# The lower part of split weights: from a subtraction on the vector engine to an accumulating DMA

## The chip, the cores and the metric

The kernel runs on one core of one Trainium2 chip. The metric is the time of an execution on the device, in microseconds (us); several executions are timed and the median stands for them.

## What is computed

Two transformer blocks follow each other over 512 tokens of 1024 features, all in float32:

```python
def reference(x, mem, ...):
    y = first_block(x, mem, ...)     # mixer, attention to 256 memory rows, gated FFN, norm
    return second_block(y, ...)      # stick-breaking attention + 31-tap conv, gated FFN

# first block
xn = rmsnorm(h, norm_mix_g);  proj = xn @ w_in
h = h + concat([pool_mixer(p), sgu_mixer(u, v)]) @ w_out
h = h + mem_cross_attention(rmsnorm(h, norm_xattn_g), mem, wq, wk, wv, wo)
h = h + (silu(gate) * val) @ w_down       # gate, val: a 3-tap convolution of xn @ w_up
# second block
proj = rms_norm(x) @ w_in_2               # q, k, v and the two halves of a gated unit
x = x + concat([attention(q, k, v), conv_branch]) @ w_out_2
x = x + (silu(conv(gate)) * val) @ w_down_2
```

What matters here is the products with weights: w_in, w_out, wq, wk, wv, wo, w_up, w_down and those of the second block, some 112 MB read once.

## The kernel before

**Products in three parts.** The matmuls take their operands in a rounded 32-bit type (`F32R`). To keep float32 accuracy, each operand is split in two, a rounded upper part `hi` and what the rounding left, `lo = raw - hi`. A product is then three matmuls into one PSUM tile, in `mm3` (L123 to L125): `wh*xh`, `wh*xl`, `wl*xh`.

**Weight units.** The weights are cut into units of 128 partitions x 2048 columns (8 KB to a partition, 1 MB in all), listed in `PLAN` in the order of use: 111 units, 8 of them with only 1536 columns (the last six of the 22 feature chunks of each down projection, `PARTS`), and three `EARLY` units that are split ahead into slots that lie free. A unit with 512 tokens takes 16 steps of `mm3`, 48 matmuls; one with 1536 columns takes 36.

**prep** (from L174) loads the next unit and splits it. Per unit:

```python
raw = wp.tile([P, UNIT], F32, tag="raw")      # pool wp: two buffers for each tag
hi = slot(..) if slots else wp.tile(.., tag="whi")
lo = slot(..) if slots else wp.tile(.., tag="wlo")
sp.dma_start(out=raw[:, cs], in_=wts[i][:, cs])                              # L190
act.copy(hi[:, cs], raw[:, cs])                                              # L197
dve.tensor_tensor(lo[:, cs], raw[:, cs], hi[:, cs].bitcast(F32), subtract)   # L198
```

Unit 0 is loaded in five pieces and its upper part is cast on VectorE (DVE, L195), with the parts of the first activations between the pieces. For all others ScalarE (ACT) casts, then DVE subtracts.

**weights** calls `prep` until two units are ready and gives out the first. So the split of unit n+1 stands in the program just ahead of the matmuls of unit n, and it writes into the whi and wlo buffers that unit n-1 used. Its raw buffer is loaded as soon as the split of unit n-1 has read it.

**Order of work.** The program is written stage by stage; each engine's order is set by a scheduler that runs a timeline of its own when the program is built (`schedule_with_timeline_sim`). An engine takes its instructions strictly in that order; each waits for its semaphores. SyncE's queue (SP) holds nearly only the weight loads. GpSimd (POOL) holds sums of squares for the norms (L301 to L305), small powers (L326, L739) and memsets in the feed-forward evacuation (L650, L992).

**Stages**, in order of time: pool and gating mixer; keys of the memory (wk); w_out; queries (wq); scores, values (wv), output (wo); feed-forward of block 1 (`ffn`: eight up units, eight up, four down, six up, four down, four down of 1536 columns, during which early units are split); gated unit, heads and convolution of block 2; attention; w_out_2; feed-forward of block 2. In an up stage the evacuation of a unit is one product on DVE (L651), taps on ACT and DVE (L128, L646), Silu (L656), a product (L657) and a split of the result (L131, L132).

Of the kernel before, what the change touches and what calls it, by code (L numbers as in the profile page):

```python
# [10 lines left out]
F32 = mybir.dt.float32  # L11
F32R = mybir.dt.float32r
AF = mybir.ActivationFunctionType
# [15 lines left out]
NWARM = 14  # L29
NFIRST = 56  # the columns of the small arrays that are needed first  # L30
PIECES = ((0, 1), (1, 2), (2, 4), (4, 6), (6, 8))


def _plan():
    """The weight units in the order in which they are used: (array, kind, place)."""
    plan = []
    plan += [("w_in", "sta", (2 * u, 2 * u + 1)) for u in range(2)]
    plan += [("w_in", "mov", (1024, 4 * h)) for h in range(2)]
    plan += [("w_in", "sta", (4 + 2 * u, 5 + 2 * u)) for u in range(2)]
    plan += [("wk", "sta", (2 * u, 2 * u + 1)) for u in range(4)]  # L40
    plan += [("w_out", "sta", (2 * u, 2 * u + 1)) for u in range(4)]
    plan += [("wq", "sta", (2 * u, 2 * u + 1)) for u in range(4)]
    plan += [("wv", "mov", (512 * c, 4 * h)) for c in range(2) for h in range(2)]
    plan += [("wo", "sta", (2 * u, 2 * u + 1)) for u in range(4)]

    def ffn(up, down):
        ups = [[(up, "sta", (i, NF + i)) for i in range(f0, f0 + n)] for f0, n in PARTS]
        dns = [[(down, "dwn", (2 * u, f0, n)) for u in range(4)] for f0, n in PARTS]
        return ups[0] + ups[1] + dns[0] + ups[2] + dns[1] + dns[2]

    plan += ffn("w_up", "w_down")
    glu = [[("w_in_2", "sta", (12 + i, 16 + i))] for i in range(4)]
    qkv = [[("w_in_2", "mov", (512 * c, 4 * h)) for h in range(2)] for c in range(3)]
    plan += glu[0] + glu[1] + glu[2] + qkv[1][1:] + glu[3] + qkv[2]
    plan += [("w_out_2", "hlf", (n0, k0)) for k0 in (0, 4) for n0 in (0, 4)]
    plan += ffn("w_up_2", "w_down_2")
    return plan, qkv[0] + qkv[1][:1]
# [18 lines left out]
def block_kernel(  # L76
# [20 lines left out]

# [1 line left out]
    def pair():  # L99
# [51 lines left out]
    class Chunks:  # L151
        """Chunks of w columns in 8 KB slots; a slice of chunks lies in one of them."""

# [16 lines left out]

# [1 line left out]
    state = {"next": 0, "ready": [], "bank": 0}  # L172

    def prep(pieces=((0, 8),), before=None, between=None, early=None, slots=None):  # L174
        """Loads and splits the next unit, or one of those that are split early into slots."""
        i = state["next"] if early is None else len(PLAN) + early
# [14 lines left out]
        for a, b in pieces:  # L191
            cs = slice(a * n // 8, b * n // 8)
            if between:
                between(a, b)
                dve.tensor_copy(hi[:, cs], raw[:, cs])  # L195
            else:
                act.copy(hi[:, cs], raw[:, cs])  # L197
            dve.tensor_tensor(lo[:, cs], raw[:, cs], hi[:, cs].bitcast(F32), ALU.subtract)  # L198
        if kind == "hlf":
# [14 lines left out]
    def sta_unit(xh, xl, nk=KC, apart=False):  # L214
        """Two 128-column tiles of a weight against the activations: out^T in a pair of banks."""
        wh, wl = weights()
        pt = [single() for _ in range(2)] if apart else pair()
        order = [(k, j) for j in range(2) for k in range(nk)]
        for k, j in order if apart else sorted(order):
            mm3(pt[j] if apart else pt[:, j, :], wh[:, k, j, :], wl[:, k, j, :], xh[:, k, :],  # L220
                xl[:, k, :], k == 0, k == nk - 1)
        return pt

    def mov_stage(xh, xl, nt, early=()):
        """512 columns of a weight against the activations: tokens on the partitions."""
        pts = [pair() for _ in range((nt + 1) // 2)]
# [11 lines left out]

# [1 line left out]
    sm = const.tile([P, NSMALL], F32, tag="sm", name="sm")  # L240
# [27 lines left out]
    dve.tensor_copy(identr, ident)  # L268
    # the tensor engine's clock rises with its use: keep it at work until the data comes
    warm = single()  # L270
    for _ in range(NWARM):
        pe.matmul(warm.rearrange("p (a b) -> p a b", a=4), negone, over2(negone, 4),
                  start=True, stop=True)
    # where a key is not before its query
    never = const.tile([P, P], F32R, tag="never", name="never")
# [5 lines left out]

# [1 line left out]
    class Stats:  # L283
        """Sums of squares over the features; parts of 1024 columns: n chunks of w tokens."""

# [43 lines left out]
    def spread(c, w=T):  # L329
        """Per-token numbers, a token to a partition, onto all partitions along the free axis."""  # L330
        nt = w // P
# [9 lines left out]

# [1 line left out]
    xh, xl = whole("B"), whole("C")  # L343
# [140 lines left out]
    def residual(xh, xl, nxt_h, nxt_l, g, nk=KC):  # L484
        """h += W^T x; the next stage's input and the sums of squares as the chunks come."""
        st = Stats()
# [11 lines left out]

# [1 line left out]
    qh, ql = whole("B"), whole("C")  # L500
# [94 lines left out]

# [1 line left out]
    def ffn(xh, xl, st, places, evacuate, finish, meanwhile=(), last=None):  # L597
# [83 lines left out]

# [1 line left out]
    cc = part(ht[0], 4, 544)  # L683
# [65 lines left out]

# [1 line left out]
    # one head pair: the logits lie transposed, keys on the partitions  # L751
    # a step takes one or two tiles of 128 keys; the columns of a tile are the queries from its
    # first key on
    STEPS = ((2, 3), (1,), (0,))
    WIDE = (384, 384, 512)

    def cols_of(a):
        """Where a tile's columns lie in its step."""
        at = 256 if a == 3 else 0
        return slice(at, at + T - a * P)  # L760
# [3 lines left out]
    def sticks(hp, n):  # L764
        """Logits of a step's keys and log(1 + e^z) of them, in two parts."""
        w = WIDE[n]
# [18 lines left out]
    def breaks(hp, n):  # L785
        """What is left of the stick at each key, and the values taken by it."""
        w = WIDE[n]
# [13 lines left out]
    def gather(hp):  # L801
        """The values of a head pair, weighted."""
        o = single(0)
# [8 lines left out]

# [1 line left out]
    done = [0] * 4  # L814
    tap = None

    def conv(n, *chunks):
        """The next n taps of some chunks, in turns: a sum's next term waits for the one before."""
        nonlocal tap
# [35 lines left out]
    def blk(hp, n):  # L855
        """Where the two parts of a step's log(1 + e^z) lie."""
        tl = place((hp % 2, 2, 3)[n])
        return tuple(part(tl, 2, WIDE[n], 2 * WIDE[n] * i) for i in range(2))

    def taken(hp, n):  # L860
        """Where a step's weights lie."""
        at = (0, 1024 * (hp % 2), 768)[n]
# [10 lines left out]
    def conv_norm():  # L873
        """The layer norm over the channels, and its output's two parts."""
        nonlocal cl
# [41 lines left out]
    def half_out(u, xh, xl, out, after=None):  # L917
        """Two column tiles of the output projection over four chunks of its input."""
        if u % 2 == 0:
# [25 lines left out]
    def project():  # L945
        """The values of all heads, a tile of tokens at a time."""
        ws = [weights() for _ in range(2)]
# [13 lines left out]
    for i, x in enumerate(seq):  # L961
        # a step's parts may be overwritten once the last step of the pair before has read them
        while todo < len(seq) and todo <= i + 2 and not (x[1] == 2 and seq[todo][1] == 1):
# [7 lines left out]
    conv_norm()  # L971
    # the tensor engine takes the norm's sums between these products
    after = (None, None, (marks[0], marks[1]), (marks[1], marks[2]))
# [45 lines left out]
def _pack(a):  # L1019
    """Inputs laid out for the kernel: transposed activations, weights in the order of use."""  # L1020
    a = {k: np.asarray(v) for k, v in a.items()}
# [77 lines left out]
```

## Time and profile before

| | |
|---|---|
| three runs | 1300.12, 1303.54, 1305.39 us; median 1303.54 |
| profiled execution: span from first to last instruction | 1301.2 us |
| TensorE matmul (PE), busy | 1282.9 us, 99% |
| VectorE (DVE) | 777.4 us, 60% |
| ScalarE (ACT) | 483.6 us, 37% |
| GpSimd (POOL) | 119.6 us, 9% |
| moved by DMA | 118.33 MB, mean 91 GB/s |
| mean granted TensorE clock | 0.990 |

The profiled execution is one more run of the same program; the page gives its span, which lies between the lowest and the median run. "PEld" in the profile is the load of the stationary operand, which overlaps PE. A busy share says how long an engine had an instruction in hand, not that it set the end; the chain of waits is there for that. Lines (L198) are those of the listing above.

### The profile page before, as it was taken

The page shows a single profiled execution, that of the slowest core. Times are in us where ns is not written, and L with a number is a line of the kernel's source. Part 1 is how long each engine was busy: PE and PEld are TensorE (multiplying, and loading weights), DVE is VectorE, ACT ScalarE, POOL GpSimd, SP SyncE. Part 2 cuts the span into 40 slices and gives each one's busy share as a digit, 9 for nine tenths or more (in the row PEclk, how much of TensorE's full clock was granted, in tenths as well). Part 3 has the DMA queues.
Part 4 walks back from the last instruction along what each step waited for, and adds up shares of the span by engine and source line. Part 5 has one row for each costly group of instructions (what it writes and reads, how often), then busy time and mean ns, then how long its engine had stood idle before and what let it go on. Part 6 is the DMA issues. An engine that isn't in the chain of part 4 may idle for free.

```text
span 1301.2 us, 13631 instructions
## 1 busy us (share of the span) xinstructions
PE 1282.9 (99%) x5712; PEld 1027.5 (79%) x5712; DVE 777.4 (60%) x811; ACT 483.6 (37%) x523; POOL 119.6 (9%) x132
## 2 busy tenths in 40 slices
PE   8999999999999999999999899999999999999998
PEld 5789888788888888888888687667878888888887
DVE  8755534744866664465476998766665555445522
ACT  5332424632544442333352225654433333223310
POOL 4100210012000000000064230000400000000000
PEclk9999999999999999999999899989999999999999
DMA  7223222312222222222442002001222222222222
GB/s 259 97 97 130 97 97 68 127 65 97 98 97 90 84 88 95 97 97 89 138 156 71 33 33 70 28 1 37 93 97 97 97 97 97 98 96 83 87 72 85
DMA packets 20446, 118.33 MB, mean 91 GB/s; under 512 B 2208, under 2 KB 4128, under 8 KB 7712
## 3 DMA queue, kind: packets, MB, share of 16 engines
q1 hardware_dynamic: 20096, 117.20, 25.9%
q8 instruction: 45, 0.74, 0.2%
q10 hardware_dynamic: 288, 0.26, 0.1%
q14 instruction: 17, 0.14, 0.0%
HBM read 115.35 MB, written 2.10 MB: 90 GB/s over the span
## 4 chain that ended last, share of the span: by engine, by line
PE 94%; DVE 3%; ACT 1%; POOL 1%; DMA 0%; issue 0%; SPq 0%; DVEq 0%; ACTq 0%
PE pp L123 29%; PE pp L124 28%; PE pp L125 28%; DVE H L828 1%; PE ps L124 1%; PE ps L123 1%; PE ps L125 1%; PE ps L809 1%; PE pp L794 1%; PE pp L797 1%; PE pp L776 1%; DMA raw<-in_wts 0%; POOL col L739 0%; PE ps L318 0%; DVE wlo L198 0%
## 5 line engine op out<-in xcount | busy, mean ns | idle before, releaser
L197 ACT CAST whi<-raw 128x2048 fp32r<-128x2048 f32 (+1 forms) x104 | 195.1, 1877 | 458.7 <-PE pp L124 376.3
L198 DVE TENSOR_TENSOR wlo<-raw,whi 128x2048 fp32r<-128x2048 f32 (+3 forms) x109 | 237.9, 2183 | 73.3 <-ACT whi L197 72.8
L124 PE MATMUL pp<-C,whi 128*128 128x512 f32 x672 | 266.2, 396 | 2.2 <-DVE C L140 2.1
L125 PE MATMUL pp<-B,wlo 128*128 128x512 f32 x672 | 266.3, 396 | 1.4 <-DVE wlo L198 1.2
L123 PE MATMUL pp<-B,whi 128*128 128x512 f32 x672 | 266.4, 397 | 0.6 <-DVE whi L195 0.4
L124 PE MATMUL pp<-G,whi 128*128 128x512 f32 x448 | 177.9, 397 | 0.0
L125 PE MATMUL pp<-F,wlo 128*128 128x512 f32 x416 | 165.0, 397 | 0.0
L123 PE MATMUL pp<-F,whi 128*128 128x512 f32 x416 | 164.2, 396 | 0.0
L124 PEld LDWEIGHTS pp<-C,whi 128*128 128x128 f32 x672 | 126.3, 188 | 34.8 <-DVE C L140 4.4
L125 PEld LDWEIGHTS pp<-B,wlo 128*128 128x128 f32 x672 | 126.2, 188 | 32.7 <-DVE wlo L198 2.3
L123 PEld LDWEIGHTS pp<-B,whi 128*128 128x128 f32 x672 | 126.3, 188 | 32.3 <-ACT B L139 1.3
L124 PEld LDWEIGHTS pp<-G,whi 128*128 128x128 f32 x448 | 84.2, 188 | 20.4 <-issue 0.5
L625 DVE TENSOR_TENSOR A<-pp,A 128x1024 f32<-128x1024 f32 x23 | 28.2, 1225 | 112.2 <-PE pp L125 112.2
L123 PEld LDWEIGHTS pp<-F,whi 128*128 128x128 f32 x416 | 78.2, 188 | 19.3 <-issue 0.2
L646 DVE SCALAR_TENSOR_TENSOR H<-H,sm,H 128x512 f32<-128x512 f32 x132 | 92.8, 747 | 0.7
L125 PEld LDWEIGHTS pp<-F,wlo 128*128 128x128 f32 x416 | 78.2, 188 | 18.9 <-issue 0.2
L828 DVE SCALAR_TENSOR_TENSOR H<-H,sm,H 128x512 f32<-128x512 f32 x120 | 90.3, 784 | 1.2
L651 DVE TENSOR_TENSOR H<-pp,rb 128x1024 f32<-128x1024 f32 x22 | 26.9, 1224 | 56.2 <-PE pp L125 49.9
L128 ACT ACTIVATE H<-H,sm 128x512 f32<-128x512 f32 x70 | 54.2, 807 | 7.5 <-DVE H L698 7.5
L993 DVE TENSOR_TENSOR H<-pp,rb 128x512 f32<-128x512 f32 x22 | 15.2, 692 | 67.6 <-PE pp L125 61.2
L124 PE MATMUL pp<-E,whi 128*128 128x512 f32 x112 | 44.4, 396 | 0.0
L123 PE MATMUL pp<-D,whi 128*128 128x512 f32 x112 | 44.2, 395 | 0.0
(295 smaller groups left out, 1881.1 us busy)
## 6 DMA issues: line engine op xcount, KB each, us to landing
raw<-in_wts SPq DMA_DIRECT2D x99, 1024.0 KB, 4.7
raw<-in_wts SPq DMA_DIRECT2D x8, 768.0 KB, 3.9
A<-in_xT SPq DMA_DIRECT2D x3, 512.0 KB, 6.8
out<-A SPq DMA_DIRECT2D x3, 512.0 KB, 2.8
D<-in_memT SPq DMA_DIRECT2D x1, 1024.0 KB, 10.8
raw<-in_wts SPq DMA_DIRECT2D x3, 256.0 KB, 7.0
A<-in_xT SPq DMA_DIRECT2D x2, 256.0 KB, 3.9
raw<-in_wts SPq DMA_DIRECT2D x2, 128.0 KB, 4.0
```

Of the source, the lines that this page charges most:

```text
L123: pe.matmul(out, wh, xh, start=start, stop=False, **kw)
L124: pe.matmul(out, wh, xl, start=False, stop=False, **kw)
L125: pe.matmul(out, wl, xh, start=False, stop=stop, **kw)
L128: act.activation(out, in_, AF.Identity, scale=scale, bias=bias)
L197: act.copy(hi[:, cs], raw[:, cs])
L198: dve.tensor_tensor(lo[:, cs], raw[:, cs], hi[:, cs].bitcast(F32), ALU.subtract)
L625: dve.tensor_tensor(hu, pt, hu, ALU.add)
L646: dve.scalar_tensor_tensor(dst, hs[:, k : k + 512], w(k), dst, ALU.mult, ALU.add)
L651: dve.tensor_tensor(hs[:, :, 2:], pt, over2(rb), ALU.mult)
L776: pe.matmul(out[:, :P], identr, never, start=False, stop=False, skip_group_check=True)
L828: tap = dve.scalar_tensor_tensor(cv[:, i, :], cc[:, i, k : k + 512], par("dw_w", 4 * k + i), cv[:, i, :], ALU.mult, ALU.add)
L993: dve.tensor_tensor(hs[:, 2:514], pt[:, 0, :], rb, ALU.mult)
```

## The change

In `prep`, on the branch that all units but unit 0 take, the subtraction on DVE goes. ACT writes the negated copy of the raw weights into lo, in the rounded type, so that lo holds -hi. ACT casts hi as before. Then POOL issues a DMA from raw to lo, both in SBUF, that adds what it reads to what is there: lo becomes raw - hi. Unit 0 keeps its way. The rest of the difference between the files is comments, which shift the line numbers: L197 becomes L200, and the negation is L199, the DMA L201.

```diff
             if between:
                 between(a, b)
                 dve.tensor_copy(hi[:, cs], raw[:, cs])
+                dve.tensor_tensor(lo[:, cs], raw[:, cs], hi[:, cs].bitcast(F32), ALU.subtract)
             else:
+
+                act.activation(lo[:, cs], raw[:, cs], AF.Copy, scale=-1.0)
                 act.copy(hi[:, cs], raw[:, cs])
-            dve.tensor_tensor(lo[:, cs], raw[:, cs], hi[:, cs].bitcast(F32), ALU.subtract)
+                pool.dma_start(out=lo[:, cs].bitcast(F32), in_=raw[:, cs], accum_op=ALU.add)
```

The scheduler sets the order anew. In the up stage of block 1, ACT's order before (whi, wlo and raw are the weight buffers, H the work tiles of the evacuation, D its output):

```order
L197 CAST whi_2365<-raw_2364 128x2048
L131 CAST D0_2141<-t2_2283 128x512
L128 ACTIVATE H1_2138<-H0_2137,sm_73 128x512 x2
```

and now:

```order
L131 CAST D0_2167<-t2_2311 128x512
L200 CAST whi_2394<-raw_2393 128x2048
L199 ACTIVATE wlo_2395<-raw_2393 128x2048
L128 ACTIVATE H1_2164<-H0_2163,sm_73 128x512 x2
L659 ACTIVATE H1_2164<-H1_2164 128x512
L131 CAST D0_2167<-t2_2380 128x512
L200 CAST whi_2463<-raw_2462 128x2048
L199 ACTIVATE wlo_2464<-raw_2462 128x2048
```

The cast keeps its place; the negation stands behind it, though the program has it ahead, and ahead of the evacuation's work.

POOL's order at the start of the program, now (acc holds the first norm's sums of squares, t4 the squares, G0 a mask, rc1 the norm's root; wlo_162 is unit 1's lower part):

```order
L304 TENSOR_TENSOR acc_175<-t4_173 128x512
L307 TENSOR_TENSOR acc_175<-acc_175,t4_177 128x512
L308 TENSOR_TENSOR acc_175<-acc_175,t4_177 128x512
L307 TENSOR_TENSOR acc_175<-acc_175,t4_181 128x512
L373 MEMSET t4_255 128x2x16
L308 TENSOR_TENSOR acc_175<-acc_175,t4_181 128x512
L307 TENSOR_TENSOR acc_175<-acc_175,t4_185 128x512
L308 TENSOR_TENSOR acc_175<-acc_175,t4_185 128x512
L201 DMA wlo_162<-raw_160 128x2048
L408 AFFINE_SELECT G0_169<-G0_169 128x512
L329 TENSOR_TENSOR rc1_247<-col4_245,mhalf_85 128x4
L201 DMA wlo_276<-raw_274 128x2048
```

Unit 1's DMA stands behind all sums of the first norm.

PE's order between the second and the third wk unit, before (H are the split memory rows; G and D belong to the gating mixer):

```order
L123 MATMUL pp_795<-H0_462,whi_738 128x256
L124 MATMUL pp_795<-H1_463,whi_738 128x256
L123 MATMUL pp_908<-G1_461,D0_493 128x128
...
L125 MATMUL pp_908<-G1_461,D1_494 128x128
L125 MATMUL pp_795<-H0_462,wlo_739 128x256
```

and now:

```order
L123 MATMUL pp_803<-H0_466,whi_745 128x256
L124 MATMUL pp_803<-H1_467,whi_745 128x256
L123 MATMUL pp_918<-G1_465,D0_497 128x128
...
L124 MATMUL pp_949<-G1_465,D0_497 128x128
L125 MATMUL pp_803<-H0_466,wlo_746 128x256
```

Before, 9 of the gating mixer's 48 short matmuls stand there and 39 behind the fourth wk unit; now 47 stand there and one behind.

## Rows read from the trace of the kernel before

**Rows 1.** The page: busy time by engine, and the chain by engine.
```profile
PE 1282.9 (99%) x5712; PEld 1027.5 (79%) x5712; DVE 777.4 (60%) x811; ACT 483.6 (37%) x523; POOL 119.6 (9%) x132
...
PE 94%; DVE 3%; ACT 1%; POOL 1%; DMA 0%; issue 0%; SPq 0%; DVEq 0%; ACTq 0%
```
**Rows 2.** Stretches of an up stage: length, busy us (instructions), clock, DMA share, GB/s.
```profile
400.00:411.20 11.20, 11.20 (x50) 9.02 (x49) 7.55 (x9) 4.59 (x5) 0.10 (x1) 1.00 0.30 100
411.20:422.40 11.20, 11.20 (x50) 9.01 (x49) 7.55 (x9) 4.58 (x5) 0.10 (x1) 1.00 0.26 91
```
**Rows 3.** PE's waits: for whom, us in total, times, longest.
```profile
PE pp L745 <- DVE D L741: 5.0, 2, 3.3
...
PE pp L125 <- DVE wlo L198: 1.2, 1, 1.2
```
**Rows 4.** Groups by form: the cast and the subtraction; busy us, mean ns, idle before.
```profile
L197 ACT CAST whi<-raw 128x2048 fp32r<-128x2048 f32 x96 | 183.3, 1910 | 415.6 <-PE pp L124 336.7 <-issue 72.8 <-DMA raw<-in_wts 5.2
...
L197 ACT CAST whi<-raw 128x1536 fp32r<-128x1536 f32 x8 | 11.9, 1482 | 43.0 <-PE pp L124 39.6 <-issue 3.4
...
L198 DVE TENSOR_TENSOR wlo<-raw,whi 128x2048 fp32r<-128x2048 f32 x96 | 219.8, 2291 | 72.9 <-ACT whi L197 72.8
...
L198 DVE TENSOR_TENSOR wlo<-raw,whi 128x1536 fp32r<-128x1536 f32 x8 | 14.1, 1757 | 0.4
```
**Rows 5.** Timeline of ACT and DVE in the up stage: start, us, what.
```profile
403.90 1.91 ACT L197 CAST whi<-raw 128x2048 fp32r<-128x2048 f32 x1 [2.86 <-PE pp L124]
...
404.16 1.23 DVE L651 TENSOR_TENSOR H<-pp,rb 128x1024 f32<-128x1024 f32 x1 [2.39 <-PE pp L125]
405.84 2.29 DVE L198 TENSOR_TENSOR wlo<-raw,whi 128x2048 fp32r<-128x2048 f32 x1 [0.46 <-ACT whi L197]
...
415.29 1.23 DVE L651 TENSOR_TENSOR H<-pp,rb 128x1024 f32<-128x1024 f32 x1 [2.33 <-PE pp L125]
```
**Rows 6.** The page's DMA issues: count, KB each, us from issue to landing.
```profile
raw<-in_wts SPq DMA_DIRECT2D x99, 1024.0 KB, 4.7
raw<-in_wts SPq DMA_DIRECT2D x8, 768.0 KB, 3.9
```
**Rows 7.** Timeline of ACT: two casts in block 1's last down stage.
```profile
647.35 1.49 ACT L197 CAST whi<-raw 128x1536 fp32r<-128x1536 f32 x1 [6.65 <-PE pp L124]
...
655.77 1.48 ACT L197 CAST whi<-raw 128x1536 fp32r<-128x1536 f32 x1 [3.42 <-issue]
```
**Rows 8.** Timeline of POOL and PE at the start.
```profile
19.62 1.62 POOL L305 TENSOR_TENSOR acc<-acc,t 128x512 f32<-128x512 f32 x1
...
27.02 0.40 PE L125 MATMUL pp<-B,wlo 128*128 128x512 f32 x1
```
**Rows 9.** Timeline of ACT and PE in the wk stage.
```profile
83.40 1.90 ACT L197 CAST whi<-raw 128x2048 fp32r<-128x2048 f32 x1 [8.38 <-issue]
...
93.29 1.91 ACT L197 CAST whi<-raw 128x2048 fp32r<-128x2048 f32 x1 [1.80 <-PE pp L124]
98.92 1.91 ACT L197 CAST whi<-raw 128x2048 fp32r<-128x2048 f32 x1 [3.73 <-PE pp L124]
...
111.49 0.27 PE L123 MATMUL pp<-G,D 128*128 128x128 f32 x1
111.60 0.27 PE L124 MATMUL pp<-G,D 128*128 128x128 f32 x1
```
**Rows 10.** Stretches: last down units of block 1; heads and convolution of block 2.
```profile
649.00:683.00 34.00, 34.00 (x147) 27.43 (x146) 26.04 (x16) 20.78 (x24) 22.19 (x13) 1.00 0.42 150
...
697.00:745.00 48.00, 43.01 (x177) 34.26 (x176) 44.40 (x46) 13.53 (x14) 19.44 (x12) 0.89 0.08 25
```
**Rows 11.** Timeline of ACT and DVE in the convolution of block 2.
```profile
700.29 0.59 ACT L339 COPY rb<-ps 128x512 f32<-128x512 f32 x1 [1.71 <-PE ps L337]
...
707.60 19.42 DVE L828 SCALAR_TENSOR_TENSOR H<-H,sm,H 128x512 f32<-128x512 f32 x21
...
740.77 2.29 DVE L198 TENSOR_TENSOR wlo<-raw,whi 128x2048 fp32r<-128x2048 f32 x1
```

## The prediction

> **What bounds the kernel now.** I read the page's busy table and chain first. PE is busy 99% of the 1301.2 us span and the chain is 94% PE [rows 1]. Then the stretch table: in periods of 11.2 us PE never rests, DVE has 7.6 us of work, ACT 4.6, and the DMA engines are 0.26 to 0.30 busy [rows 2]. Such a period is one weight unit: 48 matmuls, so 0.233 us each. The waits say how little PE waits for the operation that goes: 1.2 us for wlo in the whole run; the largest entry is 5.0 us, two waits at the head transposes [rows 3]. So the 240.8 us that DVE spends on the subtractions of the whole units (96 and 8 [rows 4], and three early ones at the same 2.29) lie beside PE's work. Taking them away can give little; what counts is whether the new way to make the lower part still fits beside PE.
>
> The cover is short. There are two buffers each of raw, whi and wlo. A unit is split into the buffers that the unit two before has just left, and must be ready when PE ends the unit between. In the up stage [rows 5] the cast starts at 403.90 and DVE reads PE's result at 404.16, so PE left the old unit at about 404.1. PE wants the new lower part one unit later, behind two matmuls with the upper part: 404.1 + 11.2 + 0.5 = 415.8. Before, it is there at 408.1: 7.7 us early.
>
> **The change, part by part.** DVE loses 240.8 us. ACT gains a second pass over each of these 107 units, priced as the cast beside it: 201 us [rows 4], so 684 us of the span, 53%. In the up stage ACT then has 6.5 of 11.2 us; this alone costs nothing, PE's work covers it. But the order puts the negation behind the cast there, so it ends at 403.9 + 2 x 1.91 = 407.7, and only then may POOL issue the accumulating DMA. **Room for the DMA: 415.8 - 407.7 = 8.1 us** from issue to landing.
>
> That DMA's time, call it A, is in no row: it reads raw, reads the negated copy, adds, writes back, and is issued by POOL, which issues no DMA now. The nearest row is the 1 MB load: 4.7 us from issue to landing [rows 6]. Lower bound: one pass like the load, 4.7. Upper bound: three passes one after the other (two reads and a write), 14.1. Splitting the load (3.1 us of engine time, which is 0.28 of 11.2 us, and 1.6 of latency) gives 1.6 + 2 x 3.1 = 7.8 if only the reading doubles. I take **9.4, the load twice**: two streams come through the same engines, and POOL's own share of the issue, unseen, has to go somewhere. The Trainium skill ("DMA: Bandwidth & Descriptors", section on the SWDGE path's anatomy) gives a DMA issued by GpSimd about 2.0 us plus its bytes at 436 GB/s. For a plain 1 MB that is 4.4 us, and the trace's 4.7 us (for a load that SP issues) agrees within 0.3. For two streams it makes 6.8 us, an estimate; by it the sum below would shrink to about nothing.
>
> When A exceeds the room by d, PE waits d in every second unit, since a buffer pair is refilled only every second unit: d/2 a unit.
> - Steady units of 11.2 us (w_out, wq, wo, both up projections, 16 whole-size down units, the output projection of block 2: 76, of which I take 72, the first of a stage having slack): 72 x (9.4 - 8.1)/2 = **47 us**.
> - The down units of 1536 columns last 8.4 us and are cast in 1.48 [rows 7]; room 8.4 + 0.5 + 0.26 - 2 x 1.48 = 6.2; their load takes 3.9 [rows 6], twice that is 7.8. Four in the second block: 4 x 0.8 = **3 us**.
> - The start: the second unit's DMA stands on POOL behind six additions, the last from 19.62 to 21.24; landing at 30.6, and PE wants it at 27.02 [rows 8]: **4 us**.
> - The memory keys (wk), with 256 memory rows, run at 5.6 us a unit [rows 9]. The second is cast from 83.40, lands at 83.4 + 3.8 + 9.4 = 96.6, and is wanted at about 93.8, as the first ends at 93.3: 2.8 us. The new order moves 38 short matmuls of 0.11 us (4.2 us) from behind the fourth to behind the second, which covers the third. The fourth is cast when the second ends (101.8), lands at 115.0, and is wanted at 113.1: 1.9. The first w_out unit, cast when the third ends (112.6), lands at 125.8; the fourth ends at 120.1, and the short matmuls that stood there are gone: 5. Together **10 us**. The wv units between the attention scores, estimated from the same 5.6 us of matmuls with other work between: **2 us**.
> - The last down stage of block 1, where early weights are split as well [rows 7]. A raw buffer now comes free only when the DMA has landed, where the subtraction freed it before. One buffer serves down units 1, 2, 3 and the first GLU unit: load 3.9, negation 1.5, DMA 7.8 make a round of 13.2 us, where PE wants a unit each 8.4. Two rounds, each 5 us late, then 4 at the GLU unit: **14 us**, 20 if loads and DMAs slow each other.
> - Returns: from 697 to 745 us DVE is busy 44.4 of 48 us and PE waits for it [rows 3, 10]. Two subtractions of 2.29 us leave it, but 21 convolution taps in a row [rows 11] still stand ahead of the reduction that PE waits for: **-3 us**, between 0 and the 5.0 us of that wait.
>
> SP's queue: each load waits for the landing in place of the subtraction; in the steady stage it has 11 us of slack and needs 4.7, so nothing. POOL's queue: its memsets and statistics sums now stand behind DMAs that wait for ACT. The memset that evacuation needs is issued after a negation that ends at 407.7, and DVE wants it at 415.3: covered. The DMA engines: 3.1 + 6.2 of 11.2 us, so not the bound at A = 9.4.
>
> Sum: 47 + 3 + 4 + 10 + 2 + 14 - 3 = +77 us on the profiled execution's 1301.2, so 1378. That span lies 2.3 us under the median of the runs shown, 1303.5; the forecast on the runs' scale is **1381 us, +5.9%**.
>
> **Rivals.**
> - *The DMA is slow.* With three passes, 14.1: 72 x 3.0 = 216, small down units 11, start 8, wk 25, wv 6, the early stage 27, less 3, together about +290: 1594. For: a read-modify-write has a store that must follow the add, where a load only stores what comes. Against: the load overlaps its reads and writes already.
> - *The DMA is quick enough*, A below the room of 8.1. At 7.8 the steady terms vanish and start 2, wk 6, early stage 8, less 3, remain: 1317. At 4.7 some 3 us of them stay and the 3 come back: 1303. For: only 0.28 of the DMA engines' time is used [rows 2]. The Trainium skill's rule quoted above speaks for this case.
> - *Faster.* One mechanism: the stretch from 697 to 745, where DVE is nearly full, PE's wait of 5.0 us is the longest of all, and the granted clock is 0.89 [rows 3, 10]. If A is under about 7, so that nothing else is late, and the taps move up by the two subtractions that are gone, that wait goes and the half-clock time behind it shrinks by perhaps 3: 1303.5 - 8 = 1295. Against: the taps there begin with the GLU product, whose input waited for a copy on ACT that ends at 700.88 [rows 11], not for the subtraction.
> - *ACT becomes the bound.* ACT's busiest stage with weights is 649 to 683 us, where it also squares for two norms: 20.8 us of 34 [rows 10], and it gets 3 x 1.91 + 1.48 = 7.2 more. Still under the stage's length; it could add some 5 us to the sum (1386), no more.
>
> **How the numbers follow.** A between 8.1 and 11 (1320 to 1455): 0.42, with ACT's 0.03 beside it. A over 11 (1455 and up, 1594 at three passes): 0.29, of which 0.10 above 1590. Quick: 0.22, of which 0.10 lands within 0.5% of before (6.5 us, about what a measurement of this kernel can tell from no change), 0.01 under that and 0.11 over it. Faster: 0.04. The range from 1305 to 1590 leaves out the 0.10 above, and about 0.09 below: the faster case and the quickest of the quick one. Slower by over 0.5%: 0.42 + 0.03 + 0.29 + 0.11 = 0.85; same 0.10; faster 0.05.
>
> **What would show it.** Right: PE's waits gain a large entry for its L125 matmuls on the accumulating DMA, about 1.3 us in every second unit of the up stage; the period there averages 11.85; the issue table shows POOL's DMAs at 8 to 11 us to landing; SP's waits name the DMA in place of the subtraction; DVE's busy time is near 540 us, ACT's near 685; single waits of some 5 us appear among the last down units of block 1. A period of 11.2 with A under 8 means the quick rival; a period near 14 the slow one. The working is wrong if PE waits instead for whi (ACT too late), or if the DMA's landing is short and its issue late, behind other work on POOL.

## The result: 5.3% slower, and not where the largest term stood

| | before | after |
|---|---|---|
| median of four runs each, side by side | 1301.83 us (1299.63 to 1305.39) | 1372.11 us (1369.65 to 1375.34) |
| ratio, 95% interval | | 1.0533 (1.0513 to 1.0553) |
| profiled span | 1301.2 us | 1370.9 us |
| mean granted TensorE clock | 0.990 | 0.971 |

The forecast was 1381 us in a range from 1305 to 1590. Time and sign came out. The way there did not: the profile denies the largest term of the sum, and holds a cost of a third of the loss that the prediction does not name.

First the page of the changed kernel, busy time and chain by engine, which answers to [rows 1], then its issue table, which answers to [rows 6].

```profile
PE 1311.5 (96%) x5712; PEld 1039.2 (76%) x5712; DVE 537.9 (39%) x704; ACT 684.9 (50%) x640; POOL 196.7 (14%) x239
...
q0 software_dynamic: 15408, 110.11, 40.2%
q1 hardware_dynamic: 20096, 117.20, 24.5%
...
PE 68%; DMA 12%; issue 9%; DVE 4%; ACT 4%; POOL 2%; SPq 0%; DVEq 0%; ACTq 0%; POOLq 0%
...
raw<-in_wts SPq DMA_DIRECT2D x99, 1024.0 KB, 4.8
wlo<-raw POOLq DMA_DIRECT2D x96, 1024.0 KB, 7.0
...
F<-raw POOLq DMA_DIRECT2D x1, 1024.0 KB, 8.9
```

DVE and ACT are as busy as forecast (540 and 685). L198 is gone, its successors are L199 and L201. DMA is 12% of the chain, where it was 0. There are 107 accumulating DMAs: `PLAN` has 105 units, not the 111 given above, and with the three early ones there are 108, of which unit 0 keeps its way. The accumulating DMA takes **7.0 us** from issue to landing (median), the prediction's A, which it put at 9.4. Its queue (q0) has 40.2% of the span for 110.11 MB, the weight loads (q1) 24.5% for 117.20 MB: per byte it holds the DMA engines 1.75 times as long as a load.

The up stage, answering to [rows 5] (timeline: start, us, engine, what, idle before), and one unit of it, answering to [rows 2]:

```profile
425.61 1.91 ACT L200 CAST whi<-raw 128x2048 fp32r<-128x2048 f32 x1 [2.48 <-PE pp L124]
425.87 1.23 DVE L654 TENSOR_TENSOR H<-pp,rb 128x1024 f32<-128x1024 f32 x1 [2.01 <-PE pp L125]
427.42 1.91 ACT L199 ACTIVATE wlo<-raw 128x2048 fp32r<-128x2048 f32 x1
...
429.62 0.86 POOL L201 DMA_DIRECT2D wlo<-raw  x1 [7.72 <-ACT wlo L199]
...
436.89 1.92 ACT L200 CAST whi<-raw 128x2048 fp32r<-128x2048 f32 x1 [2.59 <-PE pp L124]
437.08 1.22 DVE L654 TENSOR_TENSOR H<-pp,rb 128x1024 f32<-128x1024 f32 x1 [2.05 <-PE pp L125]
```

```profile
437.10:448.30 11.20, 11.20 (x49) 9.02 (x48) 5.32 (x7) 6.39 (x7) 0.95 (x2) 1.00 0.74 188
```

The period is 11.2 us as before and PE is busy for all of it. The negation ends at 429.33 and the DMA of this unit lands 6.9 us after 429.62, at 436.5. PE wants the lower part at about 437.3 (425.6 + 11.2 + 0.5): some 0.8 us are left. Such a steady unit costs nothing, though the DMA engines' share went from 0.28 to 0.74.

Where the 70 us lie shows when the start of each unit's first matmul with the lower part is taken from both traces, counted from the first matmul of the program:

| stretch | delay at its end | of it here | predicted |
|---|---|---|---|
| start and gating mixer, to the first wk unit | 4.1 | 4.1 | 4 |
| wk, to the first w_out unit | 16.2 | 12.1 | 10 |
| w_out, wq, wv, to the first wo unit | 21.0 | 4.8 | 2, and steady |
| wo and feed-forward of block 1, 34 units | 22.8 | 1.8 | steady |
| last down stage with early units, to the second GLU unit | 44.8 | 22.0 | 14 to 20 |
| heads and convolution of block 2, to the values | 40.0 | -4.8 | -3 |
| values and attention of block 2 | 64.0 | 24.0 | none |
| output projection of block 2 | 66.2 | 2.2 | steady |
| feed-forward of block 2 to its last down stage, 30 units | 68.1 | 1.9 | steady |
| last down stage of block 2 | 70.0 | 1.9 | 3 |

The steady terms were to be 47 us together. The stretches of steady units alone show 1.8 + 1.9.

Two rows need care, because the scheduler has moved work of PE across their ends. Ahead of the second GLU unit's first matmul with the lower part PE now has 3100 matmuls where it had 3075; what has moved there is ten matmuls with an early unit (F) and sixteen short ones for a norm:

```profile
722.45 0.39 PE L123 MATMUL pp<-F,B 128*128 128x512 f32 x1
...
727.55 1.84 PE L321 MATMUL ps<-ones,acc 128*128 128x1 f32 x16
```

This is work done earlier, not time lost: some 4 us of the 22.0 (10 x 0.233, and 1.7), which come back in the -4.8. At the third GLU unit, ahead of which both kernels have 3238 matmuls, the delay is 41.0. So the last down stage costs 18.2 us, and the convolution returns 1.0. In the same way 12 matmuls more (up to 2.8 us) stand ahead of the output projection of block 2; the sum of its row and the attention's, 26.2 us, does not depend on that.

PE's waits answer to [rows 3] (for whom, us in total, times, longest), with SP's largest wait below:

```profile
PE pp L125 <- DMA wlo<-raw: 20.1, 11, 4.1
PE ps L812 <- ACT B L802: 4.9, 1, 4.9
PE ps L812 <- ACT C L802: 4.7, 1, 4.7
```

```profile
SPq L190 <- DMA wlo<-raw: 1255.1, 102, 109.1
```

The wait that was forecast is there, but 11 times, not in every second of 72 units. The two entries under it belong to attention and name ACT: L802 takes the exponential of a step's weights, and has nothing to do with the lower parts.

**The last down stage of block 1**, in the chain of waits (start, us, what). F and G are the slots of two early units.

```profile
643.41 6.88 DMA wlo<-raw
650.35 4.77 DMA raw<-in_wts
655.14 1.92 ACT F L199
...
657.35 8.92 DMA F<-raw
666.31 4.75 DMA raw<-in_wts
671.08 1.91 ACT G L199
...
675.41 7.98 DMA raw<-in_wts
683.50 1.50 ACT wlo L199
...
685.29 5.75 DMA wlo<-raw
691.08 0.79 PE pp L125
```

A load follows the landing of the accumulating DMA that last read its raw buffer, as predicted. What was not: transfers that run together slow each other. The load at 675.41 takes 7.98 us in place of 4 to 5, the DMA to F 8.92 in place of 7.0; each of the two runs beside a transfer of the other kind for over 6 us.

**Attention of block 2**, ACT's timeline:

```profile
897.82 1.05 ACT L782 ACTIVATE t<-t 128x1024 f32<-128x1024 f32 x1
898.90 1.06 ACT L783 ACTIVATE t<-t 128x1024 f32<-128x1024 f32 x1
899.98 1.28 ACT L908 ACT_TABLE_LOAD   x1
901.27 0.81 ACT L908 ACTIVATE H<-H,sm 128x512 f32<-128x512 f32 x1
902.10 1.28 ACT L802 ACT_TABLE_LOAD   x1
...
904.22 1.28 ACT L908 ACT_TABLE_LOAD   x1
...
912.17 1.28 ACT L782 ACT_TABLE_LOAD   x1
...
915.06 1.28 ACT L783 ACT_TABLE_LOAD   x1
```

L908 is the Silu of the convolution's norm. Before, it ran behind the attention; now the scheduler has put it among the exponentials (L782, L802) and logarithms (L783), and each change to it or from it loads a table, 1.28 us. From 912 us on, so does each change between exponential and logarithm, which took none at 898.90. That makes 16 table loads in the program in place of 6. The Trainium skill ("ScalarE: Activation LUTs", section on what a table load costs) gives 1283 ns, as here, and adds 1380 ns of draining; these rows show none: the load starts 0.02 us after the instruction ahead of it ends, and the next instruction starts 1.29 us after the load does.

### The profile page after: what moved, and what is told of

Same layout as the page of the kernel before. It is cut to its first block, busy times and chain, and to the rows that moved or that the text cites. A ratio compares the mean times of both kernels' runs of the same rounds, so it can differ in the third digit from the quotient of the medians.

```text
span 1370.9 us, 13919 instructions
## 1 busy us (share of the span) xinstructions
PE 1311.5 (96%) x5712; PEld 1039.2 (76%) x5712; DVE 537.9 (39%) x704; ACT 684.9 (50%) x640; POOL 196.7 (14%) x239
## 3 DMA queue, kind: packets, MB, share of 16 engines
q0 software_dynamic: 15408, 110.11, 40.2%
q1 hardware_dynamic: 20096, 117.20, 24.5%
## 4 chain that ended last, share of the span: by engine, by line
PE 68%; DMA 12%; issue 9%; DVE 4%; ACT 4%; POOL 2%; SPq 0%; DVEq 0%; ACTq 0%; POOLq 0%
PE pp L125 21%; PE pp L123 21%; PE pp L124 21%; DMA wlo<-raw 9%; DMA raw<-in_wts 3%; ACT wlo L199 2%; DVE H L831 2%; PE ps L124 1%; PE ps L125 1%; POOL col L742 1%; PE ps L123 1%; DMA F<-raw 1%; PE ps L812 0%; ACT whi L200 0%; PE pp L800 0%
## 5 line engine op out<-in xcount | busy, mean ns | idle before, releaser
L200 ACT CAST whi<-raw 128x2048 fp32r<-128x2048 f32 (+1 forms) x104 | 195.0, 1876 | 396.1 <-PE pp L124 325.7
L201 POOL DMA_DIRECT2D wlo<-raw x104 | 89.8, 863 | 878.8 <-ACT wlo L199 842.3
L199 ACT ACTIVATE wlo<-raw 128x2048 fp32r<-128x2048 f32 (+1 forms) x104 | 195.2, 1877 | 25.1 <-DMA raw<-in_wts 22.2
L125 PE MATMUL pp<-D,wlo 128*128 128x512 f32 x112 | 45.9, 411 | 6.6 <-DMA wlo<-raw 6.5
## 6 DMA issues: line engine op xcount, KB each, us to landing
D<-in_memT SPq DMA_DIRECT2D x1, 1024.0 KB, 11.4
```

The source lines that it names most:

```text
L125: pe.matmul(out, wl, xh, start=False, stop=stop, **kw)
L199: act.activation(lo[:, cs], raw[:, cs], AF.Copy, scale=-1.0)
L201: pool.dma_start(out=lo[:, cs].bitcast(F32), in_=raw[:, cs], accum_op=ALU.add)
```

## The experiments

Ratios are against the kernel before on the same chip. "Delay" means what it does in the table above. In the diffs, `subtract` and `accumulate` stand for the two ways to make the lower part: the cast and DVE's subtraction of before, and the three lines of the change.

### 1. The Silu held back

```diff
+            with tc.issue_after(weighted.ins):
                 act.activation(ci, ci, AF.Silu, scale=..., bias=...)
```

`weighted` is the last exponential of the attention.

> The change, with one line of order added: the four Silu activations of the convolution's norm may not be issued before the last Exp of the attention. Theory (order): in the changed kernel the vector engine ends the convolution earlier, the scheduler moved these Silus into the attention, and ACT loads function tables 16 times in place of 6; some 20 of the 24 us lost between the projection of the values and w_out_2 come from that, so 1350 to 1357 us here, with 6 table loads. Rival (late weights): the loss in this stretch is the wait for wlo of the values' and w_out_2's units; then 1370 to 1375.

Measured: 1353.84 us, ratio 1.0405 (1.0375 to 1.0435). The same stretch around the attention (us, PE, PEld, DVE, ACT, POOL busy, clock, DMA share, GB/s), in the changed kernel:

```profile
786.00:936.00 150.00, 135.56 (x582) 96.89 (x580) 102.27 (x134) 95.55 (x104) 12.80 (x14) 0.87 0.23 61
```

and with the Silu held back:

```profile
786.00:936.00 150.00, 145.76 (x659) 105.60 (x658) 101.31 (x132) 85.52 (x97) 12.77 (x14) 0.95 0.22 57
```

PE gets 77 more matmuls done in these 150 us and the mean granted clock is 0.95 in place of 0.87 (of the two levels, 2.4 and 1.2 GHz, it spends less time at the lower). All lower parts are made as in the change, and 18 of the 70 us are gone by the medians: they came from the order of ACT's work, not from late weights. From the values to the end of the output projection the delay grows by 6.0 us in place of 26.2. The two traces also differ by 4.2 us ahead of the first wo unit, most of it at wk. There the order is the same on every engine, so this is no effect of the edit; experiments 5 and 6 have the larger delay there, 10 the smaller.

### 2. ACT's second pass kept, the sum on DVE

```diff
-                pool.dma_start(out=lo[:, cs].bitcast(F32), in_=raw[:, cs], accum_op=ALU.add)
+                dve.tensor_tensor(lo[:, cs], raw[:, cs], lo[:, cs].bitcast(F32), ALU.add)
```

> ACT's negated copy stays, but DVE adds raw to it in place of the DMA. Theory (the DMA's latency, and the raw buffer that it holds): ACT's second pass alone is covered everywhere; 1303 to 1312 us, DVE near 775 us busy, ACT near 685. Rival (ACT): the second pass on ACT, 201 us, makes the waits at wk and in the last down stage of block 1; then 1335 or more, and those stages keep their delays of 12 and 22 us.

Measured: 1303.40 us, ratio 1.0010 (0.9995 to 1.0025). The page and the group of the new addition:

```profile
PE 1283.6 (99%) x5712; PEld 1027.8 (79%) x5712; DVE 774.0 (59%) x811; ACT 671.9 (52%) x630; POOL 122.1 (9%) x132
```

```profile
L201 DVE TENSOR_TENSOR wlo<-raw,wlo 128x2048 fp32r<-128x2048 f32 x96 | 220.9, 2301 | 179.1 <-ACT wlo L199 179.0
```

ACT is nearly as full as in the change, and PE as busy as before. The second pass costs nothing, in the last down stage neither: the delay is 1.2 us at its first unit and 1.2 at the third GLU unit. The rival of ACT as the bound falls. What is lost comes with the DMA, 7.0 us in place of 2.3 for the same sum, and with the order that the scheduler set for it (there are 6 table loads here, as before).

### 3. A delay ahead of each DMA

```diff
+                pool.tensor_scalar(lo[:, :1024], lo[:, :1024].bitcast(F32), 1.0, None, ALU.mult)
                 pool.dma_start(out=lo[:, cs].bitcast(F32), in_=raw[:, cs], accum_op=ALU.add)
```

> The change, and ahead of each DMA a pass of POOL over half of wlo, multiplying it by one in place, so that the DMA is issued some 2 to 3 us later and nothing else changes. Theory (room of 8.1 us against a DMA of 7.0, with 0.3 us to its issue: 0.8 us to spare in the up stage): PE waits (2.8 - 0.8)/2 = 1.0 us a unit in the 72 steady units, the period goes from 11.2 to 12.2 us, and the short stages lose some 10 us more: 1445 to 1465 us. Rival (the steady units have more cover than these 0.8 us): under 1395.

Measured: 1537.6 us, ratio 1.1804 (1.1769 to 1.1839): on the side of the theory, but 73 to 93 us more. The negation and POOL's timeline in the up stage:

```profile
458.75 1.91 ACT L199 ACTIVATE wlo<-raw 128x2048 fp32r<-128x2048 f32 x1
460.75 2.77 POOL L201 TENSOR_SCALAR wlo<-wlo 128x1024 fp32r<-128x1024 f32 x1 [10.80 <-ACT wlo L199]
464.44 0.10 POOL L654 MEMSET H<- 128x4 f32 x1 [0.92 <-ACT H L660]
464.95 0.90 POOL L202 DMA_DIRECT2D wlo<-raw  x1 [0.41 <-POOL H L654]
```

The pass is 2.77 us, about as assumed, but the evacuation's memset has slipped between pass and DMA and waits for the evacuation's Silu on ACT. The negation ends at 460.66 (458.75 + 1.91), so the DMA starts 4.3 us after it, 4.0 later than in the changed kernel. Less the 0.8 us that were left, PE should wait 3.2. Its rows, and three stretches, the first that of the wait (columns as in experiment 1):

```profile
468.36 0.39 PE L124 MATMUL pp<-G,whi 128*128 128x512 f32 x1
472.08 0.77 PE L125 MATMUL pp<-F,wlo 128*128 128x512 f32 x1 [3.34 <-DMA wlo<-raw]
```

```profile
468.75:472.08 3.33, 0.00 (x0) 0.03 (x1) 0.80 (x1) 3.33 (x3) 0.14 (x1) 0.95 0.78 157
472.08:475.08 3.00, 3.00 (x7) 2.42 (x8) 2.43 (x4) 1.38 (x3) 2.62 (x1) 0.50 0.69 208
475.08:478.08 3.00, 3.00 (x14) 2.39 (x14) 1.80 (x3) 1.04 (x2) 1.00 (x2) 0.99 0.58 191
```

PE waits 3.34 us. Then the clock stands at 0.50 (1.2 GHz) for 3 us, in which 7 matmuls start where the next 3 us have 14: another 1.5 us. A pair of units here is some 5 us late (3.5 at the first, 1.5 at the second), which is the wait and its echo. So the prediction's rule, d every second unit, holds as to the wait in this stage, and lacks the clock. In the feed-forward of block 2 less is lost, 34 us over 30 units where 60 were lost over the same units in block 1; why is not shown.

### 4. The accumulating DMA in the up units alone

```diff
-            else:
+            elif kind == "sta" and _ in ("w_up", "w_up_2"):   # accumulate
+            else:                                             # subtract
```

> The DMA for the 44 units of the two up projections alone; all other units by the subtraction, as before. Theory: in the up stage the DMA is fully covered, and nothing is gained by a vector engine that nobody waits for: 1299 to 1308 us, within 0.5% of before, with the period at 11.2 us. Rival (the DMA or ACT's second pass costs PE something in every unit, by ports or queues): 44 of 105 units carry 40% of the loss, 1330 us.

Measured: 1310.77 us, ratio 1.0062 (1.0042 to 1.0082); 44 DMAs of 7.0 us. This is above the theory's numbers, by 2.8 us. The delays place the loss: 1.6 us up to the end of block 1, 1.7 from there to the first unit of the output projection, 4.4 at the first two up units of block 2, whose lower parts are made during the output projection, and some 1.1 later on. Inside a stage the units are nearly free, at the edge of block 2's they are not.

### 5 to 7. The edges given back, one after the other

All three have the Silu of experiment 1. In 5 the early units subtract:

```diff
+            elif early is None:                               # accumulate
+            else:                                             # subtract
```

> The changed kernel with the Silu order of the first experiment, and the three early units back on the subtraction by the vector engine; all others keep the accumulating DMA. Against 1353.8 us with the Silu order alone. Theory (in the last down stage of block 1 the loads and the accumulating DMAs of the six-chunk units and of the early units hold the two raw buffers and slow each other, 8 us instead of 4 to 5 for a load, 8.9 instead of 7.0 for an accumulating DMA): taking the early DMAs away frees one buffer and ends the collisions, but a six-chunk unit's round, load 4.1, two passes 3.0, DMA 5.9, is still 13 us against PE's 8.4; about half of the 20 us stays: 1341 to 1347. Rival 1 (the early DMAs are all of it): 1331 to 1336. Rival 2 (the six-chunk units' own DMAs are all of it): 1351 to 1356.

Measured: 1345.38 us, ratio 1.0335 (1.0315 to 1.0355), inside the theory's numbers. In 6 the six-chunk down units of block 1 subtract as well:

```diff
+            elif early is None and not (n < UNIT and _ == "w_down"):   # accumulate
```

> As the one before, and the six-chunk down units of block 1 back on the subtraction too. Theory (the delay of the last down stage of block 1, 22 us by the traces, comes from accumulating DMAs there and from nothing else): 1331 to 1336. Rival (part of the delay comes from the scalar engine's second pass or from a changed order there, and stays): 1340 or more.

Measured: 1345.13 us, ratio 1.0335 (1.0310 to 1.0360). PE's wait for the accumulating DMA between 640 and 720 us, in experiment 1, 5 and 6 (us, times, longest):

```profile
PE pp L125 <- DMA wlo<-raw: 9.1, 3, 4.0
```

```profile
PE pp L125 <- DMA wlo<-raw: 6.3, 4, 2.2
```

```profile
PE pp L125 <- DMA wlo<-raw: 1.9, 1, 1.9
```

From the first six-chunk unit to the third GLU unit, ahead of which all these programs have the same number of matmuls, the delay grows by 19.2, 10.0 and 2.2 us. So the early DMAs account for about half of it and the six-chunk units' own for two fifths. The 2.2 us that stay lie at the GLU units, whose own DMAs are still there. As to the stage the theory of 6 holds; its total, some 10 us too low, misses for two other reasons. From the values to the end of the output projection the delay grows by 12.1 us, where experiment 1 has 6.0. PE's waits for lower parts there are 5.0 us in place of 2.9; the rest is open. And 4.4 us more than in experiment 1 arise on the way to the first wo unit, where the order is the same in both. In 7 the start, wk, the first w_out unit, wq, wv and both six-chunk stages subtract too:

```diff
+            elif early is None and i >= 11 and n == UNIT and _ != "wv" and _ != "wq":   # accumulate
```

> The accumulating DMA only for units of 2048 columns from the second w_out unit on, without wq, wv and the early units: 75 units in place of 107; the subtraction for the rest; the Silu order of the first experiment. Theory (steady units hide the DMA, so what is left is what the traces show at the edges of the feed-forward stages, 3 to 8 us, less the 4 to 5 us won in the convolution of block 2): 1303 to 1311. Rival (every unit on the DMA costs its share, and the loss goes with their number: 75 of 107 units keep 0.7 of the 52 us that are left with the Silu order): 1335 or more.

Measured: 1328.65 us, ratio 1.0205 (1.0180 to 1.0229), between the two; it has 78 units on the DMA, not 75. Start and wk cost nothing now (delay -0.3 at the first w_out unit). Of the 26.3 us that the trace still loses, 4.8 lie at the other w_out units, 3.1 between the last down stage and the third GLU unit (1.4 of them come back in the convolution), and 15.7 from the values to the end of the output projection. These 15.7 are over half of the loss; PE's waits for lower parts explain 4.9 of them, the rest is open.

### 8. The accumulating DMA in the convolution alone

```diff
+            elif _ == "w_in_2" and early is None and place in ((14, 18), (512, 4), (15, 19)):   # accumulate
```

> The accumulating DMA for three units alone, those that are split while the vector engine is full with the convolution of block 2; the subtraction for all others; the Silu order of the first experiment. Theory (there the vector engine sets the pace, and the changed kernel gained 4.8 us in that stage): 1297 to 1300, faster than before by 0.25 to 0.45%. Rival (the gain there needs other units off the vector engine too, or is given back in the attention behind it): 1302 to 1305.

Measured: 1301.09 us, ratio 0.9996 (0.9985 to 1.0007): no difference. PE's first wait is that of [rows 3], at the head transposes:

```profile
PE pp L750 <- DVE D L746: 5.1, 2, 3.4
```

It was 5.0 us, longest 3.3. Three subtractions less on a full DVE do not shorten it, and the delay over the convolution moves by 0.4 us, to the worse. So the 4.8 us that the changed kernel gains in that stretch are no work saved: they are for the most part the matmuls moved ahead of the second GLU unit. In experiments 1, 5, 6, 7 and 10, 25 to 27 matmuls have moved there, and 4.6 to 7.4 us come back behind it; in experiment 2, where DVE has as much to do as before, 8 have, and 3.1 us come back; in 8 and 9 none has, and 0.4 us at most. PE's waits for DVE in that stage of the changed kernel are 3.4 and 1.3 us, hardly less than the 5.0 of before. Counted from the third GLU unit on, 1.0 us of the 4.8 is left, and 0.8 to 3.2 in experiments 1, 5, 6, 7 and 10; why is open.

### 9. The steady units alone

```diff
+            elif early is None and n == UNIT and (28 <= i < 60 or 73 <= i):   # accumulate
```

> The accumulating DMA only inside the feed-forward stages: the up units from the third on and the down units of 2048 columns, 56 of 107 units; the subtraction for all others; the Silu order of the first experiment. Theory (a steady unit of 11.2 us hides the DMA: landing 7.0 us after an issue that has 8 us of room): within 0.4% of before, 1301 to 1307, and the timeline's units start no more than 3 us later from the third up unit to the end of the down stage. Rival (the loss goes with the number of units: 52 us x 56/107): 1326 or more.

Measured: 1303.81 us, ratio 1.0023 (1.0008 to 1.0037). PE's wait, and 301 us of the feed-forward of block 1 (columns as in experiment 1):

```profile
PE pp L125 <- DMA wlo<-raw: 2.0, 3, 0.8
```

```profile
336.00:637.00 301.00, 300.30 (x1286) 241.10 (x1285) 119.26 (x149) 153.44 (x134) 24.36 (x45) 1.00 0.73 187
```

56 of the 107 units are on the DMA, and cost 1.3 us in block 1 and 2.1 in block 2. A loss by the number of units would have been 27 us.

### 10. The attention's weights

```diff
+            elif not (early is None and 65 <= i < 71):   # accumulate
```

> The changed kernel with the Silu order of the first experiment, and the six units that are split around the attention of block 2 (two of the values, four of its output projection) back on the subtraction; all others keep the accumulating DMA. Against 1353.8 us with the Silu order alone. Theory (with the table switches gone, the 6 us still lost between the values and the output projection come from late lower parts: waits of 2.5 us and less): 1346 to 1349. Rival (they come from another order of the attention's work): 1352 to 1356.

Measured: 1347.04 us, ratio 1.0355 (1.0321 to 1.0388), inside the theory's numbers, though its interval meets that of experiment 1 (1.0375 to 1.0435). The delays are clearer: from the values to the end of the output projection they stay at 32.2 and 32.1 us, where experiment 1 goes from 37.7 to 43.7.

## Why the prediction was right, and where it was not

- **The bound and the cover: right.** PE sets the time, DVE's 240 us were worth nothing, and what counts is whether the new lower part comes in time. Experiment 8, where subtractions leave DVE at its fullest and nothing is gained, shows the first half, experiments 2 and 9, where lower parts in time cost next to nothing, the second.
- **The room of 8.1 us: right.** The landing at 436.5 with 0.8 us to spare, and PE's 3.34 us behind a DMA that starts 4.0 us later, give it again.
- **The step that failed is A, "9.4, the load twice".** It is 7.0 us. Steady units thus lose almost nothing, and the 47 us, the largest term, are 3.7 in the two feed-forward stretches. The queue's 40.2% of 1370.9 us, over 105 MB-units (110.11 MB), are 5.25 us of engine time for each; 1.75 are left for latency, about the load's 1.6. Read so, the fixed part comes once, and the load's 3.1 us of engine time grow by the factor 1.7. The estimate of 6.8 us from the Trainium skill ("DMA: Bandwidth & Descriptors", section on the SWDGE path's anatomy), with the bytes counted twice, is within 0.2 us of the trace.
- **The rival of the quick DMA had its condition met (A below 8.1) and its time, 1303 to 1317, is wrong by 55 us.** Some 20 of them are the order of ACT's work (see below). For the rest, it let the edges shrink with A: wk 6 us, the early stage 8. They measured 12.1 and 18.2, near the sum with 9.4. There A is not 7.0: accumulating DMAs and loads run together, up to 11.4 us for the one and up to 9.6 for the other. The trace's mean of a steady stage is no price for a stage with transfers in a row.
- **A cost was not seen: the order of work.** 26.2 us in the attention and the output projection behind it, of which experiment 1 takes away 20.2 by the traces and 18 by the medians, and experiment 10 the rest. The order of ACT in the changed program was there to be read; the prediction read it in the up stage, at the start and at wk, and not where tables change.
- **The start, 4 us, and the last stage of block 2, 3 us: right** (4.1 and 1.9). wk came out at 12.1 for 10, and at 9 in the traces of experiments 1 and 10, which have the same order there; w_out, wq and wv lost 4.8 us where 2 were put on wv. The last down stage of block 1, 18.2 us, lies within its 14 to 20.
- **The return of 3 us: wrong.** Experiment 8 shows that none comes from the subtractions that leave DVE; the table's 4.8 us are mostly matmuls that were done earlier.
- **The signs.** Right: DVE, ACT, SP's wait, waits in the last down stage (4.0 us for 5). Wrong: the period of 11.85 us, the wait in every second unit, 8 to 11 us to landing.

So 1381 against 1372 is the sum of 43 us too much in steady units and 36 too little in the attention and at the edges. That the time came out is luck: the prediction gave 1320 to 1455 us to an A between 8.1 and 11, and A is 7.0. Open: why the scheduler moved the Silu when DVE's work shrank, and how the loss at the early units divides between the raw buffer that is held longer and the transfers that collide. A third raw buffer might tell these two apart; it was not tried. No version here beats the kernel before: the two that keep the DMA where it is free (8 and 9) end within 0.4% of it.

## What to carry to other kernels

When a step moves from an engine to a DMA, compare its landing with the time until the data is wanted, stage by stage: here it was all but free where the period was long, and the loss collected where units were short, where a stage began, and where a source buffer that had been freed by an instruction was held until a landing. Compare two traces only at points ahead of which both have the same work. A scheduler that sets the order anew can cost as much as the edit: look for what moved in the order of every engine, and count the table loads on ACT.

## What the hardware showed beyond what was expected

- A wait of PE costs more than its length: 3.34 us without work were followed by 3 us at half clock (0.50, then 0.99), 1.5 us more.
- An accumulating DMA from SBUF to SBUF of 1 MB takes 6.9 to 7.0 us for the most part in a steady stage, where it hardly meets a load, with 0.86 us of POOL to issue it. About one in six takes 7.4 to 8.2 us there (8.2 for the one issued at 597.93); why is open. Where it runs beside a load for over 4 us it takes 8.1 to 11.4 (some of these overlap another accumulating DMA too). The chain at wk shows one of the longest, and the load behind it:

```profile
109.16 11.31 DMA wlo<-raw
120.52 9.09 DMA raw<-in_wts
129.71 1.91 ACT whi L200
```
